# A decoder layer on one core: constants placed later, activation tables ordered, head sums in two float32r parts, values turned and then centred

## The chip, the core and the metric

The kernel runs on one core of one Trainium2 chip. The metric is the device time of one execution in microseconds (us), the median of several runs. The engines are PE (TensorE, matmuls; PEld is its weight load), DVE (VectorE), ACT (ScalarE), POOL (GpSimd) and SP (SyncE, here the queue of most DMAs). Each engine runs its own instructions strictly in the order in which they stand; engines wait for one another by semaphores.

## The reference

One decoder layer over 256 tokens of width 2048 in float32: a SwiGLU feed-forward, a mixer (sliding-window attention beside an RWKV-7 time mix), cross-attention to a memory of 256 rows, a second feed-forward, a final norm. What the change touches is in the time mix and in attention's softmax (cut):

```python
kk = k * k_k
kk = kk / jnp.maximum(jnp.sqrt(jnp.sum(kk * kk, axis=-1, keepdims=True)), 1e-12)   # over 64
k = k * (1.0 + (a - 1.0) * k_a)
y = rwkv7_scan(r, decay, k, v, -kk, kk * a)
mean = jnp.mean(y, axis=-1, keepdims=True)
var = jnp.mean(jnp.square(y - mean), axis=-1, keepdims=True)
y = ((y - mean) * lax.rsqrt(var + GN_EPS)).reshape(B, T, RWKV_WIDTH) * ln_w + ln_b
bonus = jnp.sum(r * k * r_k, axis=-1, keepdims=True) * v
y = (y + bonus.reshape(B, T, RWKV_WIDTH)) * g
```

A head has 64 features. Three sums over a head's features are formed: of `kk * kk`, of `r * k * r_k`, and of `y * y` (with `y` centred).

## The kernel before

**Products.** Every large product takes its float32 operands as two float32r parts: `hi` (a copy rounded to float32r by ACT, L343) and `lo` (the rest, by DVE, L344), and adds three float32r matmuls, hi x hi, lo x hi, hi x lo (L436, L437, L438). Weights stream from HBM in tiles `raw` of 2 x 128 rows by 512 columns (`load`, by SP's queue); `next_item` hands out one tile after the other, loads ahead and has the next two split (`AHEAD = 2`). One such tile is 12 matmuls on PE: two row blocks, two halves of the tokens, three parts. `feed_forward` runs over three groups of columns with seven-product combinations in place of eight (L363 to L370); its first block ends with Silu at L603.

**Background work.** All else (norms, transposes, softmax, the time mix) is written as generators in groups (`Interleave`): after every few matmuls `bg.tick()` moves each group on by one `yield`; `idle(n)` lets n ticks pass, `wait_for(name)` waits for a flag. That gives the program's order. A scheduler then places the instructions on each engine by its own costs; where `tc.issue_after(ins)` is written, what follows stays behind that instruction. A load of an activation table is put ahead of an activation whose function the table in place lacks.

**The steps touched.**
- Start: POOL makes `ones`, `ident`, masks, `bdones` (ones in two 64x64 blocks), `bdmean` (1/64 there), `bdup` (2^40 there); DVE makes `center = ident - bdmean` (L243). POOL issues DMAs for `sinks`, `g_later`, `v_rwkv` (L249, L254); ACT copies one element (L859), which brings its first table.
- `attend`: scores of 4 or 8 heads on PE (L932, L179), maxima on DVE (L959), exponentials on ACT (L965), sums and quotients on DVE (L972 to L975), `idle(4)`, transposes on PE (L187), products with `vt` (L179).
- `decay_and_rate`: per half h of the heads, products with `wa` on PE, Sigmoid on ACT (L1104), a scan on DVE (L1111), then Exp three times (L1125, L1129, L1130) and L1132.
- `removal_keys(h)`: `kk`, its square on ACT (L1148), two fp32 matmuls with `bdones` (L1153), Sqrt on ACT (L1154), reciprocals on DVE, and the products for the inverse.
- `substitute` and `invert` form the inverse of a triangular matrix in blocks: products of `xb` and `rb` (L1319), a copy `n` by ACT (L1356), products of `n` and `xu` (L1319), copies into `xb`.
- `values(h)`: eight fp32 matmuls with `center` (L1272) turn the values to tokens on partitions and centre them per head; ACT copies them to `vtok` (L1276); two fp32 matmuls with `bdones` (L1279) sum `kt` (which by then holds r * k * r_k); DVE multiplies that by the values (L1285).
- `chain(h)`: `masked` (products and a mask by DVE, L1411), `known` (L1421, copied by ACT to `u`, L1432), `solved` (L1438, L1443), `results`; `finish(h)`: square (L1517), two fp32 matmuls with `bdmean` (L1522), Sqrt (L1523), reciprocals, gate products (L1533), `yr`.

Of the kernel before, what the change touches and what calls it, by code (L numbers as in the profile page):

```python
# [142 lines left out]
def decoder_layer(ctx: ExitStack, tc: tile.TileContext, a: dict, out: bass.AP):  # L143
# [19 lines left out]
    def f32(x):  # L163
        return x.bitcast(F32)
# [57 lines left out]
    ups = cpool.tile([P, P], F32, name="ups")  # L222
    pool.memset(ups[:], UP)
    mask3 = cpool.tile([P, 3, P], F32, name="mask3")
    select(mask3[:, 0, :], ups[:], [[1, P]], ALU.is_gt, 0.0, 0, -1)
    select(mask3[:, 1, :], ups[:], [[1, P]], ALU.is_ge, 0.0, 0, -1)
    select(mask3[:, 2, :], ups[:], [[1, P]], ALU.is_ge, 0.0, 0, -1)

    mask_l = cpool.tile([P, P], F32, name="mask_l")
    select(mask_l[:], ups[:], [[-1, P]], ALU.is_gt, 0.0, 0, 1)  # L230
    bdones = cpool.tile([P, P], F32, name="bdones")
    bdmean = cpool.tile([P, P], F32, name="bdmean")
    bdup = cpool.tile([P, P], F32, name="bdup")
    pool.memset(bdones[:], 0.0)
    pool.memset(bdmean[:], 0.0)
    pool.memset(bdup[:], 0.0)
    for e in range(2):
        q = slice(64 * e, 64 * e + 64)
        pool.memset(bdones[q, q], 1.0)
        pool.memset(bdmean[q, q], 1.0 / 64)  # L240
        pool.memset(bdup[q, q], UP)
    center = cpool.tile([P, P], F32, name="center")
    dve.tensor_tensor(center[:], ident[:], bdmean[:], ALU.subtract)  # L243
# [5 lines left out]
    pool.dma_start(sinks[:], a["attn_sinks"].broadcast_to([P, 16]))  # L249
# [590 lines left out]
    with tc.tile_pool(name="f1", bufs=1, reuse_waits="tile") as sp:  # L840
        aligned(sp)
        at["pool"] = sp
        x = sp.tile([P, 2, D], F32, name="x")

        def col(n):
            return x[:, :, n * 512 : (n + 1) * 512]

        n1 = Norm(g_ffn1)
        turned = [sp.tile([P, 4, T], F32, tag="hb", name="xt", bufs=2) for _ in range(2)]
        pair = sp.tile([P, 8, T], F32, tag="thi", name="xt")  # L850
        turned = [v[:] for v in turned] + [pair[:, :4], pair[:, 4:]]
# [36 lines left out]


    with tc.tile_pool(name="mx", bufs=1, reuse_waits="tile") as sp:  # L890
# [28 lines left out]
        def attend(kvs, qb):  # L919
# [55 lines left out]
            dve.tensor_tensor(  # L975
                s3, s3, den[:].unsqueeze(2).to_broadcast([P, n, w]), ALU.mult
            )
            yield from idle(4)
            pt = t4("pt", (P, 2, 4, P))
            b = two()  # L980
            turn(
# [97 lines left out]
        def decay_and_rate():  # L1079
# [8 lines left out]
            for h in range(2):  # L1088
                cs.append(t4("cs"))
                aa.append(t4("aa"))  # L1090
                for q in (0, 2):
                    b = two()
                    by_turns(
                        (
                            b[:, e, i * T : (i + 1) * T],
                            wa[64 * e : 64 * e + 64, (4 * h + q + i) * P : (4 * h + q + i + 1) * P],
                            xwa[64 * e : 64 * e + 64, :],
                        )
                        for i in range(2) for e in (1, 0)
                    )  # L1100
                    for i in range(2):
                        for e, (dst, bias) in enumerate(((cs[h], w0), (aa[h], a0))):
                            c = 4 * h + q + i
                            act.activation(  # L1104
                                dst[:, q + i, :], b[:, e, i * T : (i + 1) * T], AF.Sigmoid,
                                bias=bias[:, c : c + 1],
                            )
                yield from idle(4)
            for h in range(2):
# [25 lines left out]

        bg.spawn("ew", decay_and_rate())
        kt = []

        def removal_keys(h):
            yield from wait_for(f"k{h}")  # L1140
# [6 lines left out]
            yield  # L1147
            act.activation(sq[:], kk[:], AF.Square)  # L1148
            yield
            b = two()  # L1150
            v = sq[:].rearrange("p (a c) t -> p a (c t)", a=2)
            for i in range(2):
                pe.matmul(b[:, i], bdones[:], v[:, i], start=True, stop=True)  # L1153
# [111 lines left out]
        def values(h):  # L1265
            yield from wait_for(f"v{h}")
            vv = bv[h]
            vtok.append(t4("vtok", (P, 2, 512)))
            b = two()
            for c in range(2):  # L1270
                for j in range(4):
                    pe.matmul(  # L1272
                        b[:, c, j * P : (j + 1) * P], vv[:, j, c * P : (c + 1) * P], center[:],
                        start=True, stop=True,
                    )
            act.copy(vtok[h][:], b[:])  # L1276
            b = two()
            for i in range(2):
                pe.matmul(  # L1279
                    b[:, i], bdones[:],  # L1280
                    kt[h][:, 2 * i : 2 * i + 2, :].rearrange("p c t -> p (c t)"),
                    start=True, stop=True,
                )
            v2 = vv[:].rearrange("p (a c) t -> p a (c t)", a=2)
            dve.tensor_tensor(v2, b[:], v2, ALU.mult)  # L1285
            yield
            bg.seen.add(f"ready{h}")

# [217 lines left out]
        def finish(h):  # L1506
# [7 lines left out]
            pool.dma_start(g2[96:, 1, :], W["rwkv_g2"][P:, f4])  # L1514
            y = yq[h]
            sq = room("sq", (P, 4, T))
            act.activation(sq[:], y[:], AF.Square)  # L1517
            yield
            b = two()
            v = sq[:].rearrange("p (a c) t -> p a (c t)", a=2)  # L1520
            for i in range(2):
                pe.matmul(b[:, i], bdmean[:], v[:, i], start=True, stop=True)  # L1522
            act.activation(v, b[:], AF.Sqrt, bias=gneps[:])  # L1523
            yield
            for i in range(4):
                dve.reciprocal(sq[:, i], sq[:, i])
# [267 lines left out]
```

## Time and profile before

| what | us |
|---|---|
| median of 3 runs (lowest, highest) | 2230.0 (2228.66, 2230.67) |
| the profiled execution | 2228.26 |
| its span, first to last instruction | 2226.5 |
| PE busy; DVE; ACT; POOL | 2212.4; 1746.7; 1193.4; 70.9 |
| mean granted TensorE clock | 0.999 |

The profile is of one execution. A timeline row reads: start, length, engine, line, operation, output <- inputs, partitions x elements, and in brackets the idle time ahead of the row and what ended it; an fp32 matmul leaves two records. A row of waits reads: who waited for whom, then the total, the number of waits and the longest. A row of stretches gives the busy time of each engine in a window.

### The profile page before, as it was taken

How to read it: one execution, taken by the hardware profiler on the slowest of the kernel's cores; microseconds unless marked ns; L12 is line 12 of the kernel's file. 1: busy time of each engine (PE TensorE's matmuls, PEld its weight loads, DVE VectorE, ACT ScalarE, POOL GpSimd, SP SyncE). 2: the span in 40 equal slices, each digit the busy share in tenths (PEclk: the TensorE clock that was granted, in tenths of full speed). 3: DMA queues.
4: the chain of work that ended last, by engine and by line, in shares of the span. 5: the costliest groups of instructions: out<-in, count | busy, mean ns of one | idle time of the engine just before them, and what ended most of it. 6: DMA issues, size and time to landing. Idle time of an engine off the chain costs nothing.

```text
span 2226.5 us, 28338 instructions
## 1 busy us (share of the span) xinstructions
PE 2212.4 (99%) x10790; PEld 1820.2 (82%) x10790; DVE 1746.7 (78%) x2038; ACT 1193.4 (54%) x1436; POOL 70.9 (3%) x139
## 2 busy tenths in 40 slices
PE   9999999999999999999999999999999999999998
PEld 7788888888888877888888888888888888888886
DVE  7988988898887567977556476558888988898887
ACT  6555555555555557544434445556555555555554
POOL 1000000000000000010400000000000000000000
PEclk9999999999999999999999999999999999999999
DMA  7566665565656544677524766557665665565564
GB/s 260 199 220 194 206 206 191 189 208 192 205 188 216 163 138 150 211 231 223 170 64 148 236 218 205 183 166 260 202 202 184 206 203 194 189 208 191 206 206 153
DMA packets 220536, 433.31 MB, mean 195 GB/s; under 512 B 13952, under 2 KB 16336, under 8 KB 220400
## 3 DMA queue, kind: packets, MB, share of 16 engines
q1 hardware_dynamic: 213200, 410.70, 55.7%
q0 software_dynamic: 6624, 20.14, 2.9%
q8 instruction: 84, 1.38, 0.3%
q10 hardware_dynamic: 576, 0.66, 0.1%
q14 instruction: 52, 0.43, 0.1%
HBM read 419.00 MB, written 12.45 MB: 194 GB/s over the span
## 4 chain that ended last, share of the span: by engine, by line
PE 97%; DVE 1%; ACT 1%; DMA 0%; issue 0%; POOLq 0%; POOL 0%; SPq 0%; ACTq 0%; DVEq 0%
PE acc L436 21%; PE acc L437 21%; PE acc L438 21%; PE two L437 9%; PE two L436 9%; PE two L438 9%; PE two L187 2%; PE two L179 1%; PE two L1319 0%; DVE lo L344 0%; PE acc L1456 0%; DMA raw<-in_ffn_w_up_dram 0%; PE acc L1438 0%; PE acc L1421 0%; PE two L1533 0%
## 5 line engine op out<-in xcount | busy, mean ns | idle before, releaser
L343 ACT CAST hi<-raw 128x1024 fp32r<-128x1024 f32 (+1 forms) x769 | 763.3, 1002 | 788.5 <-PE two L438 369.8
L344 DVE TENSOR_TENSOR lo<-raw,hi 128x1024 fp32r<-128x1024 f32 (+1 forms) x770 | 882.9, 1156 | 331.3 <-ACT hi L343 330.1
L436 PE MATMUL acc<-hi,xhi 128*128 128x512 f32 (+1 forms) x1224 | 479.4, 393 | 2.3 <-ACT hi L343 2.0
L437 PE MATMUL acc<-lo,xhi 128*128 128x512 f32 (+1 forms) x1224 | 474.8, 388 | 0.8 <-DVE lo L344 0.8
L438 PE MATMUL acc<-hi,xlo 128*128 128x512 f32 (+1 forms) x1224 | 474.0, 387 | 0.0
L436 PEld LDWEIGHTS acc<-hi,xhi 128*128 128x128 f32 x1224 | 229.7, 188 | 55.6 <-issue 5.1
L437 PEld LDWEIGHTS acc<-lo,xhi 128*128 128x128 f32 x1224 | 229.9, 188 | 49.8 <-DVE lo L344 2.8
L438 PEld LDWEIGHTS acc<-hi,xlo 128*128 128x128 f32 x1224 | 229.8, 188 | 46.3 <-DVE xlo L710 0.2
L369 DVE TENSOR_TENSOR tlo<-raw,thi 128x1024 fp32r<-128x1024 f32 x160 | 192.8, 1218 | 0.0
L368 ACT CAST thi<-raw 128x1024 fp32r<-128x1024 f32 x160 | 165.7, 1050 | 33.6 <-DVE raw L363 19.3
L437 PE MATMUL acc<-lo,hhi 128*128 128x512 f32 x424 | 166.4, 392 | 0.0
L438 PE MATMUL acc<-hi,hlo 128*128 128x512 f32 x424 | 165.2, 390 | 0.0
L436 PE MATMUL acc<-hi,hhi 128*128 128x512 f32 x424 | 159.9, 391 | 0.0
L436 PE MATMUL two<-hi,xhi 128*128 128x512 f32 x352 | 138.4, 393 | 0.0
L438 PE MATMUL two<-hi,xlo 128*128 128x512 f32 x352 | 137.1, 390 | 0.0
L437 PE MATMUL two<-lo,xhi 128*128 128x512 f32 x352 | 137.1, 389 | 0.0
L363 DVE TENSOR_TENSOR raw<-raw 128x1024 f32<-128x1024 f32 x80 | 97.4, 1217 | 14.9 <-DMA raw<-in_ffn_w_up_dram 13.8
L437 PEld LDWEIGHTS acc<-lo,hhi 128*128 128x128 f32 x424 | 79.6, 188 | 19.2 <-DVE lo L344 3.0
L436 PEld LDWEIGHTS acc<-hi,hhi 128*128 128x128 f32 x424 | 79.1, 188 | 18.9 <-ACT hi L343 2.6
L438 PEld LDWEIGHTS acc<-hi,hlo 128*128 128x128 f32 x424 | 79.6, 188 | 16.2
L436 PEld LDWEIGHTS two<-hi,xhi 128*128 128x128 f32 x352 | 66.1, 188 | 15.0 <-DVE u L588 0.5
L438 PEld LDWEIGHTS two<-hi,xlo 128*128 128x128 f32 x352 | 66.0, 188 | 13.8
(385 smaller groups left out, 3181.6 us busy)
## 6 DMA issues: line engine op xcount, KB each, us to landing
raw<-in_ffn_w_gate_dram SPq DMA_DIRECT2D x171, 512.0 KB, 3.7
raw<-in_ffn_w_up_dram SPq DMA_DIRECT2D x167, 512.0 KB, 4.6
raw<-in_ffn_w_down_dram SPq DMA_DIRECT2D x152, 512.0 KB, 4.7
raw<-in_w_in_dram SPq DMA_DIRECT2D x136, 512.0 KB, 3.6
raw<-in_w_out_dram SPq DMA_DIRECT2D x32, 512.0 KB, 4.2
raw<-in_ffn_w_down_dram SPq DMA_DIRECT2D x12, 1024.0 KB, 5.1
raw<-in_w_proj_attn_dram SPq DMA_DIRECT2D x16, 512.0 KB, 3.8
raw<-in_w_proj_rwkv_dram SPq DMA_DIRECT2D x16, 512.0 KB, 4.3
```

Of the source, the lines that this page charges most:

```text
L179: prev = pe.matmul(to, lhs, rhs, **how)
L187: prev = pe.transpose(to, src, ident[:])
L343: newest["act"] = act.copy(hi[:, s], raw[:, s])
L344: newest["dve"] = dve.tensor_tensor(lo[:, s], raw[:, s], f32(hi[:, s]), ALU.subtract)
L363: dve.tensor_tensor(ta[:], raw[:, 1:3], raw[:, 0:2], ALU.subtract)
L368: act.copy(hi[:, s], t[:])
L369: dve.tensor_tensor(lo[:, s], t[:], f32(hi[:, s]), ALU.subtract)
L436: pe.matmul(o, xh, hi, start=first, stop=False, **how)
L437: pe.matmul(o, xh, lo, start=False, stop=False, **how)
L438: newest["pe"] = pe.matmul(o, xl, hi, start=False, stop=last, **how)
```

## The change

**Constants.** The DMAs for `g_later`, `v_rwkv` and `sinks` move into the generator `late_vectors`, behind `idle(60)`. The masks are selected in place of from `ups`; `bdones` and `bdmean` become float32r; `center` goes.

**Tables.** The first activation is a Silu instead of a copy. After the copy of `q0` to `qt` a one-element Exp follows. The Exps of `decay_and_rate` are held behind the last Sigmoid. One `idle(4)` in `attend` becomes `idle(5)`.

**Head sums.** `head_sums` adds two float32r matmuls, of a high part and a low part, in place of one fp32 matmul. The high part comes from ACT (a second Square, or a copy), the low part from DVE. The parts have one buffer each (`bufs=1`), and `alone()` lets one user in at a time.

**Values.** `values` turns with transposes, then DVE sums 64 features per head and token (`vmean`) and adds -1/64 of it.

```diff
+    def by_head(name, value, dt):
+        t = cpool.tile([P, P], dt, name=name)
+        pool.memset(f32(t[:]), 0.0)
...
+    bdones = by_head("bdones", 1.0, F32R)
+    bdmean = by_head("bdmean", 1.0 / 64, F32R)
...
-    pool.dma_start(sinks[:], a["attn_sinks"].broadcast_to([P, 16]))
-    gains = vectors("g_later", 4 * KD, pool)
-    rv = vectors("v_rwkv", 83, pool)
...
     def late_vectors():
+        yield from idle(60)
+        pool.dma_start(gains[:], a["g_later"])
+        pool.dma_start(rv[:], a["v_rwkv"])
+        pool.dma_start(sinks[:], a["attn_sinks"].broadcast_to([P, 16]))
         yield from idle(20)
...
-        act.copy(junk_t[:, :1], ones[:, :1])
+        act.activation(junk_t[:, :1], ones[:, :1], AF.Silu)
...
-            act.copy(dst[:], feats(tok))
+            last = act.copy(dst[:], feats(tok))
+            if name == "q0":
+                with tc.issue_after(last.ins):
+                    act.activation(junk_t[:, :1], ones[:, :1], AF.Exp)
...
-            yield from idle(4)
+            yield from idle(5 if nk == 2 and kvs[0] else 4)
...
-                act.activation(dec[h][:], dec[h][:], AF.Exp, scale=-DECAY)
-                act.activation(e0[h][:], mid[:], AF.Exp, scale=DECAY)
-                act.activation(ee[h][:], c3, AF.Exp, scale=-DECAY)
+                with tc.issue_after(rates.ins):
+                    act.activation(dec[h][:], dec[h][:], AF.Exp, scale=-DECAY)
+                    act.activation(e0[h][:], mid[:], AF.Exp, scale=DECAY)
+                    act.activation(ee[h][:], c3, AF.Exp, scale=-DECAY)
...
+        def head_sums(bd, parts):
+            b = two()
+            for i in range(2):
+                for j, part in enumerate(parts):
+                    pe.matmul(b[:, i], bd[:], part[:, i], start=j == 0, stop=j == 1)
+            return b
+        def alone():
+            while "parts" in bg.seen:
+                yield
+            bg.seen.add("parts")
...
+            yield from alone()
+            parts = parted("sq")
+            act.activation(parts[0][:], wide4(kk), AF.Square)
             act.activation(sq[:], kk[:], AF.Square)
             yield
-            for i in range(2):
-                pe.matmul(b[:, i], bdones[:], v[:, i], start=True, stop=True)
-            act.activation(v, b[:], AF.Sqrt)
+            dve.tensor_tensor(parts[1][:], v, f32(parts[0][:]), ALU.subtract)
+            yield from idle(2)
+            act.activation(v, head_sums(bdones, parts)[:], AF.Sqrt)
+            bg.seen.discard("parts")
...
-                    pe.matmul(
-                        b[:, c, j * P : (j + 1) * P], vv[:, j, c * P : (c + 1) * P], center[:],
-                        start=True, stop=True,
+                    pe.transpose(
+                        b[:, c, j * P : (j + 1) * P], vv[:, j, c * P : (c + 1) * P], ident[:]
                     )
-            act.copy(vtok[h][:], b[:])
+            dve.tensor_reduce(vmean[h][:], b3, AX.X, ALU.add)
+            dve.scalar_tensor_tensor(
+                vtok[h][:].rearrange("p c (g f) -> p (c g) f", f=64),
+                vmean[h][:].unsqueeze(2).to_broadcast([P, 16, 64]), -1.0 / 64, b3,
+                ALU.mult, ALU.add,
+            )
+            parts = parted("sq")
+            act.copy(parts[0][:], wide4(kt[h]))
+            dve.tensor_tensor(parts[1][:], wide4(kt[h]), f32(parts[0][:]), ALU.subtract)
+            yield from idle(2)
+            dve.tensor_tensor(wide4(vv), head_sums(bdones, parts)[:], wide4(vv), ALU.mult)
```

`finish` is changed as `removal_keys` is, with `bdmean`.

**Where instructions stand.** Line numbers of the changed kernel are higher by 2 (start) to 32 (chain): its L345/L346 are the casts `hi` and `lo` (L343/L344 before), L438 to L440 the three matmuls, L1154 the matmul of `head_sums`, L1351 those of `invert`.

PE, the first inversion and the start of the first chain, before; `xb`, `rb`, `n`, `xu` are the inverse's tiles, `at`, `rt`, `aa`, `kk` those of `masked`, `vtok` and `mk` those of `known`:

```order
L1319 MATMUL two<-xb,rb 64x64 x15
L179 MATMUL two<-at,aa 128x128 x4
L437 MATMUL acc<-lo,xhi 128x512
L179 MATMUL two<-rt,aa 128x128 x8
L1319 MATMUL two<-n_8933,xu 64x64 x16
L438 MATMUL acc<-hi,xlo 128x512
L436 MATMUL acc<-hi,xhi 128x512
L437 MATMUL acc<-lo,xhi 128x512
L438 MATMUL acc<-hi,xlo 128x512
L1421 MATMUL acc<-vtok,mk 128x64 x8
```

and of the change:

```order
L1351 MATMUL two<-xb,rb 64x64 x15
L438 MATMUL acc<-hi,xhi 128x512
L439 MATMUL acc<-lo,xhi 128x512
L440 MATMUL acc<-hi,xlo 128x512
L1351 MATMUL two<-n_8989,xu 64x64 x16
L179 MATMUL two<-at,aa 128x128 x8
L179 MATMUL two<-rt,aa 128x128 x8
L1453 MATMUL acc<-vtok,mk 128x64 x8
```

The products of `masked`, which stood around the products with `rb`, now stand behind those with `xu`, right ahead of `known`.

DVE, the first softmax, between the sums of the exponentials and the quotients, before:

```order
L344 TENSOR_TENSOR lo<-raw,hi 128x1024
L974 RECIPROCAL den<-den 128x8
L974 RECIPROCAL den<-den 128x4
L975 TENSOR_TENSOR s<-s,den 128x1024 x2
L344 TENSOR_TENSOR lo<-raw,hi 128x1024 x2
```

and of the change:

```order
L346 TENSOR_TENSOR lo<-raw,hi 128x1024
L979 RECIPROCAL den<-den 128x8
L979 RECIPROCAL den<-den 128x4
L346 TENSOR_TENSOR lo<-raw,hi 128x1024
L980 TENSOR_TENSOR s<-s,den 128x1024 x2
```

One more `lo` stands ahead of the quotients; on PE the transposes behind them stand eight matmuls later. On ACT the load of Exp's table and the one-element Exp stand ahead of the cast `hi` which before stood ahead of the load.

POOL, the end of its start, of the change, with what each waits for in brackets:

```order
L245 MEMSET keep 128x2 [waits Pool_49]
L274 MEMSET gneps 128x1
L276 MEMSET nhalf 128x2
L266 DMA g_later<-in_g_later_dram 128x64
L267 DMA v_rwkv<-in_v_rwkv_dram 128x83
L268 DMA sinks<-in_attn_sinks_dram 128x16
L756 TENSOR_TENSOR rs<-ms,nhalf 128x2 [waits DVE_49,Pool_49]
```

Before, the three stood among the last memsets, ahead of `gneps`; now they stand behind all of them and ahead of the first wait for another engine.

More of the change, by code (lines that the diff above doesn't have):

```diff
@@ L220, in decoder_layer @@
     select(abias[:, 1, :], abias[:, 1, :], [[-1, P]], ALU.is_ge, NEG, 0, 1)
-    ups = cpool.tile([P, P], F32, name="ups")
-    pool.memset(ups[:], UP)
     mask3 = cpool.tile([P, 3, P], F32, name="mask3")
-    select(mask3[:, 0, :], ups[:], [[1, P]], ALU.is_gt, 0.0, 0, -1)
-    select(mask3[:, 1, :], ups[:], [[1, P]], ALU.is_ge, 0.0, 0, -1)
-    select(mask3[:, 2, :], ups[:], [[1, P]], ALU.is_ge, 0.0, 0, -1)
+    pool.memset(mask3[:], UP)
+    for m, op in enumerate((ALU.is_gt, ALU.is_ge, ALU.is_ge)):
+        select(mask3[:, m, :], mask3[:, m, :], [[1, P]], op, 0.0, 0, -1)
     mask_l = cpool.tile([P, P], F32, name="mask_l")
[L230 to L243, printed above, removed]
+    pool.memset(mask_l[:], UP)
+    select(mask_l[:], mask_l[:], [[-1, P]], ALU.is_gt, 0.0, 0, 1)
+    def by_head(name, value, dt):
+        t = cpool.tile([P, P], dt, name=name)
+        pool.memset(f32(t[:]), 0.0)
+        for e in range(2):
+            q = slice(64 * e, 64 * e + 64)
+            pool.memset(f32(t[q, q]), value)
+        return t
+    bdones = by_head("bdones", 1.0, F32R)
+    bdmean = by_head("bdmean", 1.0 / 64, F32R)
+    bdup = by_head("bdup", UP, F32)
+    vmean = [cpool.tile([P, 16], F32, name="vmean") for _ in range(2)]
     keep = cpool.tile([P, 2, P], F32, name="keep")
@@ L257, in decoder_layer @@
     g_ffn1 = vectors("g_first", KD, act)
-    gains = vectors("g_later", 4 * KD, pool)
+    gains = cpool.tile([P, 4 * KD], F32, name="g_later")
     g_mix, g_cross, g_mem, g_ffn2 = (gains[:, i * KD : (i + 1) * KD] for i in range(4))
-    rv = vectors("v_rwkv", 83, pool)
+    rv = cpool.tile([P, 83], F32, name="v_rwkv")
     w0, a0, k_k, k_a, r_k, ln_w, ln_b = (rv[:, i * 8 : (i + 1) * 8] for i in range(7))
@@ L1103, in decay_and_rate @@
                             c = 4 * h + q + i
-                            act.activation(
+                            rates = act.activation(
                                 dst[:, q + i, :], b[:, e, i * T : (i + 1) * T], AF.Sigmoid,
@@ L1137, in decoder_layer, with parted, wide4 @@
         kt = []
+        def parted(name):
+            return [
+                sp.tile([P, 2, 512], F32R, tag=name + e, name=name + e, bufs=1)
+                for e in ("hi", "lo")
+            ]
+        def head_sums(bd, parts):
[8 more added lines that the diff above has]
+            bg.seen.add("parts")
+        def wide4(x):
+            return x[:].rearrange("p (a c) t -> p a (c t)", a=2)
         def removal_keys(h):
@@ L1271, in values @@
                 for j in range(4):
-                    pe.matmul(
-                        b[:, c, j * P : (j + 1) * P], vv[:, j, c * P : (c + 1) * P], center[:],
-                        start=True, stop=True,
-                    )
-            act.copy(vtok[h][:], b[:])
[L1277 to L1285, printed above, removed]
+                    pe.transpose(
+                        b[:, c, j * P : (j + 1) * P], vv[:, j, c * P : (c + 1) * P], ident[:]
+                    )
+            b3 = b[:].rearrange("p c (g f) -> p (c g) f", f=64)
+            dve.tensor_reduce(vmean[h][:], b3, AX.X, ALU.add)
[4 more added lines that the diff above has]
+            )
+            yield from alone()
+            parts = parted("sq")
[3 more added lines that the diff above has]
+            dve.tensor_tensor(wide4(vv), head_sums(bdones, parts)[:], wide4(vv), ALU.mult)
+            bg.seen.discard("parts")
             yield
@@ L1516, in finish @@
             sq = room("sq", (P, 4, T))
+            v = wide4(sq)
+            yield from alone()
+            parts = parted("sq")
+            act.activation(parts[0][:], wide4(y), AF.Square)
             act.activation(sq[:], y[:], AF.Square)
             yield
[L1519 to L1523, printed above, removed]
+            dve.tensor_tensor(parts[1][:], v, f32(parts[0][:]), ALU.subtract)
+            yield from idle(2)
+            act.activation(v, head_sums(bdmean, parts)[:], AF.Sqrt, bias=gneps[:])
+            bg.seen.discard("parts")
             yield
```

3 lines of the change are left out of this document (1 added, 2 removed).

## The prediction

> **What bounds the kernel.** I read the page first, for the busy shares.
>
> ```profile
> span 2226.5 us, 28338 instructions
> PE 2212.4 (99%) x10790; PEld 1820.2 (82%) x10790; DVE 1746.7 (78%) x2038; ACT 1193.4 (54%) x1436; POOL 70.9 (3%) x139
> ```
>
> TensorE is busy for 99% of the span, so nearly every microsecond of its work that goes is a microsecond of the kernel. The view of waits, for TensorE alone, says how little else there is:
>
> ```profile
> PE acc L436 <- ACT hi L343: 2.0, 2, 1.3
> PE two L187 <- DVE s L975: 1.2, 2, 0.9
> PE acc L204 <- POOL ones L199: 1.1, 1, 1.1
> PE acc L437 <- DVE lo L344: 0.8, 2, 0.5
> PE two L187 <- ACT tok L905: 0.4, 1, 0.4
> PE acc L436 <- ACT xhi L709: 0.3, 1, 0.3
> ```
>
> These waits sum to 5.8 us (total, times, longest). The rest of the change (tables, constants) can win at most the part of them that it touches. The sum is made against the profiled execution, 2228.26 us; the shown runs have a median of 2230.0, so I carry the difference over to that median.
>
> **Sums over a head, and values.** Matmul records overlap, so a block is priced from its start to the start of what follows, in the timeline of TensorE. First the pace of float32r work and of eight transposes:
>
> ```profile
> 1062.12 0.40 PE L437 MATMUL acc<-lo,xhi 128*128 128x512 f32 x1
> ...
> 1083.66 1.03 PE L187 MATMUL two<-ident,tok 128*128 128x128 f32 x8
> 1084.45 0.48 PE L436 MATMUL acc<-hi,xhi 128*128 128x512 f32 x1
> 1084.77 0.40 PE L437 MATMUL acc<-lo,xhi 128*128 128x512 f32 x1
> ```
>
> Between the first two rows lie eight weight tiles of 12 matmuls less one, 95: 21.54 / 95 = 0.227 us each. Eight transposes take 0.79, and the matmul behind them 0.32 instead of 0.227: 0.88 in all. Then the blocks that the change replaces, the sum of squares of the removal keys (two fp32 matmuls, four records) and the values (eight matmuls with `center`, then two with `bdones`):
>
> ```profile
> 873.54 1.88 PE L1153 MATMUL two<-sq,bdones 128*128 128x512 f32 x4
> 874.86 0.80 PE L436 MATMUL acc<-hi,xhi 128*128 128x512 f32 x1
> 875.49 0.40 PE L437 MATMUL acc<-lo,xhi 128*128 128x512 f32 x1
> ...
> 1158.33 1.95 PE L1272 MATMUL two<-center,bv 128*128 128x128 f32 x16
> ...
> 1161.43 0.79 PE L436 MATMUL acc<-hi,xhi 128*128 128x512 f32 x1
> 1162.06 0.40 PE L437 MATMUL acc<-lo,xhi 128*128 128x512 f32 x1
> ```
>
> A head sum costs 875.49 - 873.54 - 0.227 = 1.72 us, the values 1162.06 - 1158.33 - 0.227 = 3.50. Before: four head sums alone (two of keys, two of group norm, of the same shape) and two of values, 4 x 1.72 + 2 x 3.50 = 13.9. After: six head sums of four float32r matmuls, 6 x 4 x 0.227 = 5.4, and two times eight transposes, 1.8: 7.2. TensorE is rid of **6.7 us**, 6.3 if each new block costs one more change of kind (0.09 on the way in).
>
> VectorE and ScalarE pay. VectorE gets ten more passes over 128x1024 (six low parts, two means, two subtractions), 10 x 1.22 = 12 us by the rows of the chain below; ScalarE six more and two copies fewer, about 4 us, and three table loads fewer. Both have room in these stages:
>
> ```profile
> 860.00:960.00 100.00, 100.00 (x480) 80.57 (x479) 80.52 (x82) 54.81 (x60) 8.15 (x14) 1.00 0.66 208
> 1088.00:1130.00 42.00, 41.98 (x488) 34.98 (x487) 19.64 (x24) 13.70 (x19) 6.20 (x12) 1.00 0.30 92
> ```
>
> (stretch, length, then busy us of PE, PEld, DVE, ACT, POOL.) VectorE is at 81% in the stage of the keys and 47% in the chain, ScalarE at 55% and 33%. So these passes cost nothing but where TensorE stands right behind one.
>
> It does at one place, the first inversion and chain, whose new order is shown above.
>
> ```profile
> 1106.46 0.71 PE L179 MATMUL two<-at,aa 64*128 64x128 f32 x8
> 1107.10 0.50 PE L437 MATMUL acc<-lo,xhi 128*128 128x512 f32 x1
> ...
> 1108.71 0.50 PE L1319 MATMUL two<-n,xu 64*64 64x64 f32 x5
> ...
> 1106.56 1.01 ACT L1356 COPY n<-two 64x1024 f32<-64x1024 f32 x1 [1.66 <-PE two L1319]
> ...
> 1107.22 1.22 DVE L1411 TENSOR_TENSOR mk<-two,mask 128x1024 f32<-128x1024 f32 x1 [1.87 <-PE two L179]
> ```
>
> Now: the products with `rb` end at 1106.46, ScalarE copies them until 1107.57, and the next products start at 1108.71, behind 2.25 us of other work. In the new order only three float32r matmuls stand between, 3 x 0.227 + 0.09 = 0.77, against 0.10 + 1.01 + about 0.1 that the copy takes: a wait of about 0.4. Then `masked` takes 0.12 + 1.22 + about 0.1 behind its products, and only eight short ones (1.09 us) stand before `known`: 0.3 more. I take **+0.7**; zero if the records flatter these ends, 3 if each of the chain's eight hand-overs loses as much (8 x 0.35). What waits behind is only filler of the gate product, and nothing else is late: the last `yr` part keeps more than ten weight tiles before the product that reads it.
>
> **Tables.** Three of 17 loads go. One is seen by TensorE:
>
> ```profile
> 50.75 1.28 ACT L603 ACT_TABLE_LOAD   x1
> 52.05 0.69 ACT L603 ACTIVATE hb<-acc,rs 128x512 f32<-128x512 f32 x1
> ...
> 53.72 1.04 ACT L343 CAST hi<-raw 128x1024 fp32r<-128x1024 f32 x1
> ...
> 53.27 0.69 DVE L484 TENSOR_TENSOR clo<-u,chi 128x512 fp32r<-128x512 f32 x1 [0.96 <-ACT chi L481]
> ...
> 55.48 1.22 DVE L344 TENSOR_TENSOR lo<-raw,hi 128x1024 fp32r<-128x1024 f32 x1
> ...
> 54.82 0.74 PE L436 MATMUL acc<-hi,xhi 128*128 128x512 f32 x2 [0.70 <-ACT hi L343]
> ...
> 56.75 0.50 PE L437 MATMUL acc<-lo,xhi 128*128 128x512 f32 x1 [0.49 <-DVE lo L344]
> ```
>
> The load of Silu's table holds the cast `hi` back by 1.28, which costs TensorE 0.70, and then 0.49 for `lo`. Without it `hi` is in time; `lo` stands on VectorE behind L484 and what follows it, which sat idle 0.96 for `chi`, itself behind the load. So `lo` comes about 1.0 earlier for a TensorE that comes 0.7 earlier: 0.2 of its wait stays. **-1.0**, at most -1.2, zero if `lo` is held by the passes before it. The Trainium skill (ScalarE: Activation LUTs, What ACT_TABLE_LOAD costs) counts 1.28 us for the load and 1.38 for a drain; the rows show 1.30 from the load's start to the next ACTIVATE, so the trace disagrees on the drain. By that section of the Trainium skill both waits would go whole, 1.2 instead of 1.0, and the sum would be 0.2 lower.
>
> In attention the new load of Exp's table moves work too.
>
> ```profile
> 766.87 1.05 ACT L343 CAST hi<-raw 128x1024 fp32r<-128x1024 f32 x1 [0.37 <-PE acc L438]
> 770.79 1.28 ACT L965 ACT_TABLE_LOAD   x1 [2.87 <-DVE es L962]
> ...
> 779.94 2.36 DVE L975 TENSOR_TENSOR s<-s,den 128x1024 f32<-128x1024 f32 x2
> ...
> 781.31 1.06 PE L187 MATMUL two<-ident,s 128*128 128x128 f32 x8 [0.86 <-DVE s L975]
> ...
> 817.65 1.21 DVE L975 TENSOR_TENSOR s<-s,den 128x1024 f32<-128x1024 f32 x1
> ...
> 818.98 1.04 PE L187 MATMUL two<-ident,s 128*128 128x128 f32 x8
> ```
>
> Before, the load stood in a gap of 2.87 us. Now it stands, with a dummy Exp, before the cast of 766.87, which starts about 1.1 later; its `lo` and both maxima queue behind it on VectorE, so the exponentials start about 0.95 later although no load is ahead of them. One more `lo` (1.15 net of overlap) stands before L975, and the transposes come eight matmuls (1.8) later: 0.86 + 0.95 + 1.15 - 1.8, about 1.15, 0.3 worse. The second wait on L975 (1.2 - 0.9 = 0.3) goes, since those transposes come six matmuls later. At 818.98 there was no wait, with 0.12 to spare behind L975; there one more 128x1024 `lo` is ahead of it (1.2) and TensorE comes 0.3 later: 0.75 new. The wait on `tok` (0.4) stays, 0.1 longer: less table, but six matmuls less ahead. Together **+0.8**; -1.6 if all these waits go, +2.5 if two more softmaxes lose a `lo`.
>
> **Constants.** The three DMAs are written later, but they wait for nothing and POOL has nothing before them to wait for, so POOL issues them right behind its memsets, later than now by the few short memsets that stand ahead (an estimate: 0.7 us), and past no other queue's work.
>
> ```profile
> 4.99 0.73 POOL L249 DMA_DIRECT2D sinks<-in_attn_sinks_dram  x1
> ...
> 11.71 1.99 ACT L343 CAST hi<-raw 128x1024 fp32r<-128x1024 f32 x2 [3.08 <-DMA raw<-in_ffn_w_up_dram]
> ```
>
> They share the DMA engines with the second weight tile in either order, which lands at 11.71. I take **0**, between +0.3 and -1.6 (the 1.3 on `hi` and 0.3 on `lo` that TensorE loses there). The masks, `bdones` and `center` are made under the first products: 0; without that cover some 0.5.
>
> **Sum:** -6.7 + 0.7 - 1.0 + 0.8 + 0 = -6.2, so 2222.1 for a profiled run and **2223.8 us** for the median.
>
> **Rivals.** (1) *The waits go as well*: attention loses its waits (-1.6 instead of +0.8) or the chain none: a further 0.7 (chain) to 3.1 us (both), 2220.7 to 2223.1 and about 2221. For it: the scheduler left no wait in the chain before. Against: it placed table loads and casts wrongly by 0.3 to 0.9 us before. 12%. (2) *The constants are late indeed*, and the first tile lands for an unstalled TensorE: a further -1.6, 2222.2, inside the forecast's range. The Trainium skill (DMA: Bandwidth & Descriptors, Queues, rings and completion order) has each engine take turns between queues, which no run here shows for these. 6%. (3) *VectorE gives the gain back*: its extra passes stand before `lo` in the stage of the keys, where it is at 81%, so a third to a half of the 12 us reaches TensorE: 2223.8 + 2 to 5, about 2227. Against: weights are split two tiles, 5.4 us, ahead. 14%. (4) *Slower*: the head sums' new path in the chain (cast, subtract, sums, multiply, each on another engine) becomes the bound. It decides once the ten added passes fall on TensorE's path in full, with 0.1 of hand-over each: 13 instead of 0.7, so 2223.8 + 12.5, about 2236. For it: between 1100 and 1112 few float32r matmuls fill. Against: the scheduler hoists the casts many tiles ahead. 5%. The forecast keeps 63%.
>
> **Chances.** This kernel's runs can tell some 0.2%, 4.5 us, from no change: below 2225.5 is faster, above 2234.5 slower. The forecast's own range from its terms' bounds is 2220.5 to 2227. With (1) and (2) nearly all of it is faster: 0.82; (3) and the forecast's upper end give the same, 0.13; (4) slower, 0.05. The range takes in (1) and most of (3): **2219.5 to 2228**.
>
> **What would show it.** In the profile after: blocks of four 512-wide matmuls with `bdones` or `bdmean` of 0.91 us from start to next start (wrong if near 1.7); eight transposes of the values in 0.8 to 0.9; no load and no wait near 54; waits on the softmax near 783 and 820 of about 1; two waits under 0.5 near the first chain; the constants' DMAs on POOL between 5 and 8 us and the same 1.3 wait near 12.8. It would be wrong if TensorE's waits in 860 to 1225 sum to over 3 us, or if the span fell by more than TensorE's busy time plus 3.

## The result, and the profile after

The changed kernel takes 2221.75 us (median of 6 runs, 2220.58 to 2223.26) against 2229.44 for the kernel before (6 runs): ratio 0.9965, interval 0.9952 to 0.9978, so 7.7 us less, 4.9 to 10.7. The profiled execution took 2222.56, with a span of 2220.8 against 2226.5: 5.7 less. The forecast was 2223.8 (6.2 less), in a range of 2219.5 to 2228.

The head of the page of the changed kernel, and its view of TensorE's waits (total, times, longest):

```profile
span 2220.8 us, 28313 instructions
PE 2207.0 (99%) x10774; PEld 1817.7 (82%) x10774; DVE 1759.2 (79%) x2047; ACT 1193.8 (54%) x1438; POOL 72.0 (3%) x140
...
PE acc L204 <- POOL ones L199: 1.1, 1, 1.1
PE two L187 <- ACT tok L907: 1.0, 2, 0.6
PE acc L439 <- DVE lo L346: 0.9, 2, 0.6
PE acc L438 <- ACT hi L345: 0.7, 2, 0.5
PE two L187 <- DVE s L980: 0.6, 1, 0.6
PE acc L438 <- ACT xhi L711: 0.4, 1, 0.4
PE two L1351 <- ACT n L1388: 0.2, 1, 0.2
PE two L438 <- DVE hlo L669: 0.2, 1, 0.2
```

TensorE is busy for 5.4 us less (2212.4 to 2207.0), VectorE for 12.5 more, as the forecast counted (12). The waits sum to 5.1 instead of 5.8, but they stand in other places. Both executions, cut at the same three pieces of work (the transposes of `tok` that begin attention, end it and end the mixer), show where the 5.7 came from. The columns are the stretch, its length, the busy time of PE, PEld, DVE, ACT and POOL with the number of records, then TensorE's granted clock, the DMA engines' busy share and their GB/s; first the kernel before, then the changed one:

```profile
0.00:764.42 764.42, 760.24 (x3403) 624.94 (x3404) 644.04 (x744) 420.69 (x485) 11.67 (x39) 1.00 0.61 205
764.42:853.51 89.09, 87.53 (x515) 68.12 (x514) 62.39 (x96) 57.84 (x108) 1.22 (x3) 1.00 0.44 133
853.51:1435.99 582.48, 582.46 (x3360) 482.35 (x3361) 384.58 (x442) 285.31 (x337) 48.21 (x82) 1.00 0.59 187
1435.99:2226.50 790.51, 782.13 (x3515) 644.77 (x3513) 655.67 (x757) 429.57 (x509) 9.80 (x15) 1.00 0.58 198
```

```profile
0.00:763.43 763.43, 760.76 (x3402) 624.83 (x3403) 644.11 (x743) 419.76 (x484) 12.22 (x40) 1.00 0.61 205
763.43:852.92 89.49, 87.77 (x516) 68.18 (x514) 60.95 (x95) 55.16 (x105) 1.21 (x3) 1.00 0.43 132
852.92:1430.28 577.36, 576.33 (x3344) 480.09 (x3345) 398.24 (x453) 289.16 (x343) 48.70 (x82) 1.00 0.59 188
1430.28:2220.80 790.52, 782.15 (x3515) 644.56 (x3513) 655.87 (x757) 429.72 (x509) 9.82 (x15) 1.00 0.58 198
```

The first feed-forward gives 0.99, attention costs 0.40, the time mix gives 5.12, the rest 0. In the time mix VectorE does 13.7 us more and TensorE 6.1 less. A head sum and the transposes of the values look like this in the timeline of TensorE:

```profile
877.90 0.40 PE L1154 MATMUL two<-sqhi,bdones 128*128 128x512 f32 x1
878.13 0.40 PE L1154 MATMUL two<-sqlo,bdones 128*128 128x512 f32 x1
878.37 0.39 PE L1154 MATMUL two<-sqhi,bdones 128*128 128x512 f32 x1
878.60 0.39 PE L1154 MATMUL two<-sqlo,bdones 128*128 128x512 f32 x1
878.83 0.40 PE L438 MATMUL acc<-hi,xhi 128*128 128x512 f32 x1
...
1097.21 1.04 PE L1301 MATMUL two<-ident,bv 128*128 128x128 f32 x8
1098.01 0.48 PE L438 MATMUL acc<-hi,xhi 128*128 128x512 f32 x1
1098.32 0.40 PE L439 MATMUL acc<-lo,xhi 128*128 128x512 f32 x1
```

The sum takes 878.83 - 877.90 = 0.93 in place of 1.72, the transposes 1098.32 - 1097.21 - 0.23 = 0.88.

One wait, 0.59 for `tok` at 1036.94, stands in this profile alone: in the four later profiles of kernels that keep this part or add to VectorE's work in it (E, G, H and I below) the same stage took 576.43 to 576.45 instead of 577.36, without that wait. So the change is worth about 6.0 us there. Why this one execution had the wait isn't known.

### The profile page after: what moved, and what is told of

The parts are those of the page before. It is cut to its first block, busy times and chain, and to the rows that moved or that the text cites. A ratio compares the mean times of both kernels' runs of the same rounds, so it can differ in the third digit from the quotient of the medians.

```text
span 2220.8 us, 28313 instructions
## 1 busy us (share of the span) xinstructions
PE 2207.0 (99%) x10774; PEld 1817.7 (82%) x10774; DVE 1759.2 (79%) x2047; ACT 1193.8 (54%) x1438; POOL 72.0 (3%) x140
## 3 DMA queue, kind: packets, MB, share of 16 engines
q8 instruction: 84, 1.38, 0.2%
## 4 chain that ended last, share of the span: by engine, by line
PE 96%; DVE 1%; issue 1%; ACT 1%; DMA 0%; POOLq 0%; POOL 0%; SPq 0%; ACTq 0%; DVEq 0%
PE acc L438 21%; PE acc L439 20%; PE acc L440 20%; PE two L438 9%; PE two L439 9%; PE two L440 9%; PE two L187 2%; PE two L179 1%; DVE lo L346 1%; PE two L1351 0%; PE acc L1488 0%; PE acc L1453 0%; PE acc L1470 0%; PE two L1568 0%; PE acc L1351 0%
## 5 line engine op out<-in xcount | busy, mean ns | idle before, releaser
L345 ACT CAST hi<-raw 128x1024 fp32r<-128x1024 f32 (+1 forms) x769 | 764.0, 1003 | 794.3 <-PE two L440 370.6
L346 DVE TENSOR_TENSOR lo<-raw,hi 128x1024 fp32r<-128x1024 f32 (+1 forms) x770 | 884.2, 1158 | 325.0 <-ACT hi L345 323.7
L438 PE MATMUL acc<-hi,xhi 128*128 128x512 f32 (+1 forms) x1224 | 477.9, 391 | 1.1 <-ACT hi L345 0.7
L440 PE MATMUL acc<-hi,xlo 128*128 128x512 f32 (+1 forms) x1224 | 473.8, 387 | 0.0
L438 PEld LDWEIGHTS acc<-hi,xhi 128*128 128x128 f32 x1224 | 229.6, 188 | 53.3 <-issue 3.9
L440 PEld LDWEIGHTS acc<-hi,xlo 128*128 128x128 f32 x1224 | 229.8, 188 | 46.3 <-DVE xlo L712 0.2
L440 PE MATMUL acc<-hi,hlo 128*128 128x512 f32 x424 | 165.1, 389 | 0.0
L438 PE MATMUL acc<-hi,hhi 128*128 128x512 f32 x424 | 159.8, 391 | 0.1
L438 PE MATMUL two<-hi,xhi 128*128 128x512 f32 x352 | 138.4, 393 | 0.0
L440 PE MATMUL two<-hi,xlo 128*128 128x512 f32 x352 | 137.0, 389 | 0.0
L438 PEld LDWEIGHTS acc<-hi,hhi 128*128 128x128 f32 x424 | 79.1, 188 | 18.8 <-ACT hi L345 2.6
L440 PEld LDWEIGHTS acc<-hi,hlo 128*128 128x128 f32 x424 | 79.6, 188 | 16.3
L438 PEld LDWEIGHTS two<-hi,xhi 128*128 128x128 f32 x352 | 66.1, 188 | 15.0 <-DVE u L590 0.5
L440 PEld LDWEIGHTS two<-hi,xlo 128*128 128x128 f32 x352 | 66.1, 188 | 13.9
```

The lines of the kernel that those rows point to most:

```text
L345: newest["act"] = act.copy(hi[:, s], raw[:, s])
L346: newest["dve"] = dve.tensor_tensor(lo[:, s], raw[:, s], f32(hi[:, s]), ALU.subtract)
L438: pe.matmul(o, xh, hi, start=first, stop=False, **how)
L440: newest["pe"] = pe.matmul(o, xl, hi, start=False, stop=last, **how)
```

## Experiments

Differences are of medians, each against the runs of the kernel before on the same chip (2229.4 for A to H, 2230.3 for I and J).

| kernel | median | change | ratio, interval |
|---|---|---|---|
| A sums and values alone | 2223.61 | -5.8 | 0.9975, 0.9964 to 0.9985 |
| B values alone | 2227.84 | -1.5 | 0.9992, 0.9984 to 1.0001 |
| C tables alone | 2228.45 | -0.9 | 0.9996, 0.9987 to 1.0005 |
| D constants alone | 2228.65 | -0.7 | 0.9997, 0.9988 to 1.0006 |
| E the change, constants at 92 us | 2221.65 | -7.8 | 0.9963, 0.9949 to 0.9977 |
| F before, sinks' DMA last | 2229.29 | -0.1 | 0.9998, 0.9989 to 1.0007 |
| G the change, low parts twice | 2221.36 | -8.1 | 0.9962, 0.9950 to 0.9975 |
| H the change, Exp's table earlier | 2220.88 | -8.6 | 0.9960, 0.9947 to 0.9972 |
| I as H, one more idle | 2220.31 | -10.0 | 0.9954, 0.9942 to 0.9967 |
| J the change without the idles | 2223.48 | -6.8 | 0.9968, 0.9956 to 0.9981 |

**A. Sums and values alone.** The kernel before with `head_sums`, its six users and the new `values`; `bdones` and `bdmean` become float32r in their old places.

> The kernel before with the head sums in two float32r parts and the values turned and centred; constants and tables stay. Theory (TensorE's time is rid of the fp32 matmuls, and the ten passes on VectorE are hidden): 5.4 to 6.2 us less, a median near 2223.6, and TensorE's waits in the stages of the keys and of the chain under 0.5 us. Rival (VectorE gives the gain back): 1.5 to 4 us less, with waits on lo or on the low parts of 2 us or more. Rival (the hand-overs of the chain bound it): no gain or a loss.

5.8 us less. The stage from the keys to the end of the mixer took 577.50 instead of 582.48, with 1.1 us of waits in it (0.20 for `n`, 0.87 for `mk`). No wait on a low part. The time is the theory's and both rivals fall; the theory's bound of 0.5 us on the waits is passed by the one on `mk`, which B shows too.

**B. Values alone.**

```diff
-                    pe.matmul(
...
+                    pe.transpose(
...
-            act.copy(vtok[h][:], b[:])
...
+            dve.tensor_reduce(vmean[h][:], b3, AX.X, ALU.add)
+            dve.scalar_tensor_tensor(
...
```

> The kernel before with the values turned and centred alone; the sum of r * k * r_k behind them stays in fp32. Theory: two blocks of eight fp32 matmuls of 1.78 us become eight transposes of 0.88, so 1.8 us less in TensorE's time, a median near 2227.6. The forecast's own count (3.50 us for the values with the head sum behind them, 1.72 for a head sum alone) gives the same 1.8. Rival (the two new passes of VectorE between the transposes and the chain's first product are waited for): 0 to 0.8 us less, with a wait on vtok.

TensorE's busy time in the stage fell from 582.46 to 580.67, the 1.8 expected. But one wait is new, in the timeline of TensorE (the chain of the second half):

```profile
1165.88 0.32 PE L1425 MATMUL acc<-vtok,mk 128*128 128x64 f32 x1 [0.92 <-DVE mk L1415]
```

So 0.9 of the 1.8 is given back in this profile: neither the theory nor the rival has it whole. The wait is not for `vtok` but for the mask's product, which starts on VectorE at 1164.66 behind other passes, among them the two new ones (1159.60 and 1161.87). The median's 1.5 can't decide, since its interval holds zero. With A, 1.8 of TensorE's gain is the values' and the rest the sums'.

**C. Tables alone.** The Silu, the Exp behind `q0`, the order of the Exps behind the Sigmoids and the idle of 5.

> The kernel before with the three edits on ACT's tables and the idle of 5; all else stays. Theory (the trace after): the two waits near 55 go for the most part and 0.3 to 0.5 us come back within 40 us behind them; in attention waits move but their sum stays: 0.3 to 0.9 us less in all. Forecast: 1.0 less and 0.8 more, 0.2 less in all, waits on the softmax of 1.1 and 0.75. Rival (the load with a drain): 1.2 less at the start.

The first stage took 763.47 (764.42 before), attention 89.41 (89.09): 0.6 less in these two stages, though the whole span was 0.2 longer (2226.7), by the last stage. The medians' 0.9 less has an interval that holds zero. So the time decides nothing; the rows speak for the theory. Behind the two waits near 55 TensorE is 0.97 earlier (57.60 instead of 58.57), and after a wait of 0.23 for `hlo` at 60.84 it is 0.45 earlier (61.17 instead of 61.62): the rival's 1.2 without a return isn't there.

**D, E, F. Constants.** D has the change's masks and later DMAs alone. E and F:

```diff
 # E, the change with
-        pool.dma_start(gains[:], a["g_later"])
-        pool.dma_start(rv[:], a["v_rwkv"])
-        pool.dma_start(sinks[:], a["attn_sinks"].broadcast_to([P, 16]))
+        with tc.issue_after(newest["load"].ins):
+            nc.sync.dma_start(gains[:], a["g_later"])
+            nc.sync.dma_start(rv[:], a["v_rwkv"])
+            nc.sync.dma_start(sinks[:], a["attn_sinks"].broadcast_to([P, 16]))
 # F, the kernel before with
-    pool.dma_start(sinks[:], a["attn_sinks"].broadcast_to([P, 16]))
...
     rv = vectors("v_rwkv", 83, pool)
+    pool.dma_start(sinks[:], a["attn_sinks"].broadcast_to([P, 16]))
```

> The kernel before with the constants' three DMAs written later and the masks made as in the change; sums, values and tables stay. Theory (the later issue of the sinks' DMA takes a stall out of the weight stream near 10 us): the wait on hi near 12.8 falls from 1.27 to about 0.5 and the time by 0.8 us. Rival (the forecast: three DMAs of the same kind in the same window; the stall is a chance of that one profile): a wait of 0.5 or 1.3 by chance, no change of the time within 0.5.

> The changed kernel with the three DMAs of the constants on SP's queue behind the weight loads of that place, some 40 us after the start. Theory (these DMAs stall the weight stream near 10 us): no stall of the DMA engines between 9 and 12 us, the waits of 0.49 and 0.28 near 12 and 13 gone, 0.8 us less than the changed kernel (2221.0 against 2221.8). Rival (the second weight tile is bound by its own bytes): waits of 0.5 and 0.3 again and the same time.

> The kernel before with one line moved: the sinks' DMA stands behind the two of g_later and v_rwkv instead of ahead of them, so it is issued near 6.2 us instead of 4.99; nothing else. If the sinks' 16-element rows are what stalls the weight stream, the stall moves from 9.6 to about 11 us and the wait on hi near 12.8 falls from 1.27 to 0.5 to 0.8. If it is all three, the stall stays near 10 us and the wait at 1.2 or more. The time moves by under 0.8 us either way.

The busy share of the DMA engines over the first 16 us, in 40 slices of 0.4 us (a digit is tenths): of the kernel before, with the bandwidth of each slice below it, then of F, the changed kernel, D and E in this order; in the first four also the row of POOL's queue (packets, MB, share of the 16 engines' time):

```profile
DMA  0000368989999999999999999049999999999999
GB/s 0 0 0 0 56 129 306 376 259 371 348 371 369 356 356 287 287 266 333 364 384 405 410 343 67 0 164 406 421 436 384 394 410 405 410 389 420 379 415 410
q0 software_dynamic: 96, 0.08, 7.9%
...
DMA  0000368989999999999999999997598999999999
q0 software_dynamic: 96, 0.08, 5.4%
...
DMA  0000568979999999899999999999999999999999
q0 software_dynamic: 96, 0.08, 1.7%
...
DMA  0000559989999999999999999999996989999999
q0 software_dynamic: 96, 0.08, 4.4%
...
DMA  0000648999999999999999999999999999999999
```

Before, the stream falls to 67, 0 and 164 GB/s in the slices from 9.6 to 10.8, and POOL's 96 packets take 7.9% of the engines' time; A, B and C, with the old order too, have 8.3, 7.4 and 7.7%. The queue's row for the one microsecond from 9 to 10 tells what holds the engines:

```profile
q0 software_dynamic: 16, 0.01, 104.7%
```

Sixteen packets, 0.01 MB in all as the sinks' 8 KB would be, took 104.7% of what 16 engines have in that microsecond: about a microsecond of an engine each. In F the sinks' DMA is issued last, at 6.31 instead of 4.99, with the other two ahead of it, and the dent is later too, from 10.8 to 11.6; in E, without the three, there is none. So the dent goes with the sinks' DMA. The Trainium skill (DMA: Bandwidth & Descriptors, Queues, rings and completion order) lets an engine take turns between queues by whole packets. The rows agree in that the weights stand still while such packets last; the packet's microsecond is the measurement's.

The later issue doesn't always make these packets short. With the sinks issued at 7.2 the queue's share is 1.7% in the changed kernel and in G, but 2.3 to 4.4% in J, I, H and D, and in D the stream still falls to 146 GB/s, now between 11.2 and 12.4. What the later issue does in all six is to put the dent, where there is one, behind the landing of the second weight tile.

What the dent costs is seen in that landing, read from ScalarE's first cast of the tile: 11.71, 12.02, 11.75 and 11.77 in the four kernels with the old order (before, A, B, C), 11.59 in F, 10.67 to 11.24 in the six that issue the DMAs later (D, the changed kernel, G, H, I, J), and 10.92 in E. TensorE starts its products with the tile at 12.80 to 13.12 in the first four, 12.69 in F, 11.77 to 12.34 in the six and 12.02 in E. The wait on `hi` ahead of them is a poorer measure, since TensorE doesn't come to it at the same time: 1.27 before, but 0.71 in C with the old order. F's 0.63 is what its expectation gave for the sinks, yet TensorE gains 0.11 there; F settles where the dent comes from, not what it costs. D's wait was 0.74, the changed kernel's 0.49, and E's still 0.40, though its constants were issued at 92.31, later than the 40 us that were meant. So E's rival holds: with no constants in the way the tile is no earlier than in the six, and moving them yet later brings nothing. And the 0.59 that D gained at 12 us (12.21 instead of 12.80) doesn't reach the end: D's first stage took 764.44, as before, and its median is 0.7 lower with an interval from 2.7 lower to 1.3 higher, which leaves both theory and rival of D open as to the time. In D a wait of 0.55 on a `lo` at 19.30 took it back at once; what does so in the others wasn't settled, since first stages of the same start differ by up to 1.9 us from run to run (762.30 to 764.23).

**G. Low parts twice.** Each of the six subtractions is written twice.

```diff
             dve.tensor_tensor(parts[1][:], v, f32(parts[0][:]), ALU.subtract)
+            dve.tensor_tensor(parts[1][:], v, f32(parts[0][:]), ALU.subtract)
```

> The changed kernel with each of the six low parts of the head sums formed twice (the same subtraction into the same tile), which is 6 x 1.22 = 7.3 us more on VectorE in the stages of the keys and of the chain, and nothing else. Theory (VectorE's passes are hidden): within 0.5 us of the changed kernel, with the wait on tok near 1037 of 0.6 grown to at most 1. Rival (a third to a half reaches TensorE): 2.4 to 3.7 us more.

The stage of the changed kernel (first row) and of G:

```profile
852.92:1430.28 577.36, 576.33 (x3344) 480.09 (x3345) 398.24 (x453) 289.16 (x343) 48.70 (x82) 1.00 0.59 188
...
851.72:1428.16 576.44, 576.00 (x3344) 480.25 (x3345) 404.41 (x459) 289.17 (x343) 48.70 (x82) 1.00 0.62 189
```

VectorE does 6.2 us more in six instructions more, the stage is not longer, and no wait is new; the one on `tok` near 1037, which the expectation let grow, isn't there. The cover is read off the changed kernel's rows: the first low part is formed at 869.44, and the sum that reads it starts at 877.90.

```profile
869.44 1.23 DVE L1180 TENSOR_TENSOR sqlo<-sq,sqhi 128x1024 fp32r<-128x1024 f32 x1 [0.68 <-ACT sq L1178]
```

**H, I. Attention.** H loads Exp's table behind another copy; I also changes one idle.

```diff
 # H and I
-            if name == "q0":
+            if name == "kv":
 # I alone
-            yield from idle(5 if nk == 2 and kvs[0] else 4)
+            yield from idle(5 if kvs[0] == 2 else 4)
```

> The changed kernel with the one-element Exp behind the copy of kv instead of that of q0, some 22 us earlier, where ScalarE idles 1.66 us between casts. Theory (the load delays the cast ahead of the maxima by 1.1, and the softmax with it): the exponentials start 1.0 earlier, the waits of 0.60 and 0.61 near 778 and 819 go for the most part: 0.8 to 1.2 us less than the changed kernel. Rival (VectorE's passes ahead of the quotients set these waits): under 0.3 us less, waits in the same places.

> The changed kernel with the one-element Exp behind the copy of kv, and the idle of 5 also given to the single head group that follows (kvs[0] == 2), which puts its eight transposes two matmuls later. Theory: the wait of 0.60 near 818 shrinks by 2 x 0.23 to about 0.15, no other wait grows: 0.4 to 0.5 less than with the preload alone (2220.4 against 2220.9), 1.3 less than the changed kernel. Rival (the products behind the transposes are waited for instead): no change against the preload alone.

The changed kernel's load, the cast that it delays, the first exponential, the three waits of the stage (ScalarE and TensorE):

```profile
765.54 1.28 ACT L917 ACT_TABLE_LOAD   x1
766.84 0.20 ACT L917 ACTIVATE junk<-ones 128x1 bf16<-128x1 f32 x1
766.95 1.03 ACT L345 CAST hi<-raw 128x1024 fp32r<-128x1024 f32 x1
771.88 2.91 ACT L970 ACTIVATE s<-two,nm 128x128 f32<-128x128 f32 x10 [3.90 <-DVE es L967]
778.35 0.50 PE L439 MATMUL acc<-lo,xhi 128*128 128x512 f32 x1 [0.60 <-DVE lo L346]
818.81 1.06 PE L187 MATMUL two<-ident,s 128*128 128x128 f32 x8 [0.61 <-DVE s L980]
852.92 1.09 PE L187 MATMUL two<-ident,tok 128*128 128x128 f32 x8 [0.44 <-ACT tok L907]
```

and of H, whose attention also starts at 763.43:

```profile
742.87 1.28 ACT L917 ACT_TABLE_LOAD   x1
769.82 2.18 ACT L970 ACTIVATE s<-two,nm 128x128 f32<-128x128 f32 x8 [2.89 <-DVE es L967]
817.85 1.06 PE L187 MATMUL two<-ident,s 128*128 128x128 f32 x8 [0.60 <-DVE s L980]
```

The exponentials start 2.06 earlier (the theory had 1.0), the wait at 778 is gone, and attention takes 88.49 instead of 89.49. The wait near 818 stays at 0.60: there the rival is right, VectorE's passes ahead of the quotients set it. In I, whose transposes come two matmuls later, it is 0.34, and attention takes 87.89. Theory and rival each had one wait. I has the lowest median of all kernels tried; its interval and the changed kernel's overlap, so only the trace tells them apart.

**J. Without the idles.** `yield from idle(2)` ahead of each head sum goes (three places, six sums).

> The changed kernel without the idle of 2 between the low part and the head sum at its three places (six sums in all). It asks what hides the path square, square, subtract (1.0 + 1.0 + 1.2 us) ahead of each sum. Theory (the matmuls that the two ticks leave between hide it): TensorE waits 0.5 to 2 us at each of the sums, 3 to 10 us more than the changed kernel. Rival (the scheduler, which orders by its own costs, keeps work between in any case): within 0.7 us of the changed kernel and no new wait over 0.5.

No sum waits. The first one starts at 875.04, its low part (870.19) long done: the scheduler leaves work between of its own accord. The stage takes 577.03, 0.6 more than in E, G, H and I; its one wait of weight is in the second chain, while the 0.2 for `n` is gone:

```profile
1163.31 0.88 PE L1451 MATMUL acc<-vtok,mk 128*128 128x64 f32 x6 [0.91 <-DVE mk L1441]
```

It is the wait of A and B, from another order. By the ratios J is 0.7 us behind the changed kernel, inside the intervals, as the rival had it but for the one wait.

## Why the prediction held, step by step

| term | forecast | trace |
|---|---|---|
| sums and values on TensorE | -6.7 | -6.5 |
| waits and restarts in the chain | +0.7 | +0.4 |
| Silu's table | -1.0 | -0.5 to -0.8 |
| attention | +0.8 | +0.4 |
| constants | 0 | -0.8 at 12 us; in D 0 at the end of the stage |

The first two rows are the busy time and the rest of the stage in E, G, H and I (582.46 to 576.0, and 0.02 to 0.44). They give -6.0 in sum, just the forecast's, though each is smaller than forecast. The third is what stands at 60 us in the changed kernel (below), and C's first stage, 763.47, against 764.42, 764.47 and 763.83 in the three executions with the old start (before, A, B), mean 764.24; such stages scatter by as much. Silu's gain came out 0.2 to 0.5 smaller than forecast and attention's loss 0.4 smaller: that these two misses cancel is luck, and so is a total this close to the forecast.

- **Sums and values** were priced right, block by block (0.93 for 0.91, 0.88 for 0.88). The missing 0.2 stands at the two sums with fp32 products beside them, 1.11 at 1108.55 and 1.03 at 1172.08; the other four take 0.93 or 0.94.
- **The chain** waits at the first of the two places named, 0.21 instead of 0.4; behind `masked` it doesn't wait in the changed order, though in A, B and J the second chain does, by 0.9. The mechanism was right; the size depends on an order that the forecast could only read for one kernel.
- **Silu's table:** the direct gain is as forecast. Against its old place TensorE stands 1.81 earlier at 56.76, of which 0.78 had come by 12.02: 1.03. C is 0.97 earlier at the same row, having come 0.07 later to its place near 12.8: 1.04. The forecast missed what was late next: the products at 59.98, which wait for `hlo` and didn't wait before (61.39).

```profile
53.54 0.73 PE L438 MATMUL acc<-hi,xhi 128*128 128x512 f32 x2 [0.21 <-ACT hi L345]
56.76 0.48 PE L438 MATMUL two<-thi,chi 128*128 128x512 f32 x1
58.70 1.22 DVE L669 TENSOR_TENSOR hlo<-two,hhi 128x1024 fp32r<-128x1024 f32 x1
59.98 0.50 PE L438 MATMUL two<-hi,chi 128*128 128x512 f32 x1 [0.20 <-DVE hlo L669]
```

  One row further on TensorE is 1.3 earlier instead of 1.8 (0.2 of wait and the start again behind it). The Trainium skill (ScalarE: Activation LUTs, What ACT_TABLE_LOAD costs) counts a drain of 1.38 us beside the load of 1.28. The changed kernel's rows of 765.54 and 766.84, like those of before, show 1.30 from the load's start to the next ACTIVATE: no such drain shows here.
- **Attention:** the delay of the cast, and with it of the exponentials, was as argued (H shows it: the wait goes with the delay). But the forecast put the first wait at the transposes, 1.15; it came 3.8 us earlier, 0.60 at a `lo` that stands behind the sums of the exponentials on VectorE, and after it the transposes were in time. A lateness is paid where it is met first. The second, 0.75, was 0.61, and `tok` 0.44.
- **Constants:** the step that failed is that the DMAs "share the DMA engines with the second weight tile in either order", so that the wait of 1.3 stays. It fell to 0.49. The forecast had the issue times nearly right for two of the three, but the sinks went from first to last, 4.99 to 7.21, and it took all three for equal: in the old order the sinks' packets last a microsecond each and stand ahead of the tile's landing, in the new one they come behind it. The size was inside the bound (-1.6). In D the gain is lost again before the stage ends; in the changed kernel what is left of it can't be told from the scatter.
- **Rivals:** (1) the waits go as well: some did, some came. (2), the constants late and their stall gone, came true in part: the dent came behind the tile's landing, but that gave 0.8 at 12 us instead of 1.6, and E shows that no more is to be had. (3) is refuted by G, (4) by A and J.
- **Sums of the prediction:** three don't come out as written. The bounds of its terms, added up, give 2218.9 to 2229.5 and not 2220.5 to 2227; a third to a half of 12 us is 4 to 6 and not 2 to 5 (rival 3); and eight new blocks at 0.09 each would be 0.7 and not 0.4. The forecast of 2223.8 rests on none of them.

The forecast's 6.2 lies within the measured 4.9 to 10.7, which is too wide to judge the small terms. A, C and D together give 7.4, C and D with intervals that hold zero.

## What to carry to other kernels

Where one engine is busy for 99%, price each of its blocks from start to next start and count on that; here the sum was right to 0.2 us in 6.7, and the passes handed to an engine at 80% cost nothing as long as they stand microseconds ahead of their reader (in B two of them stood right ahead of a product that TensorE needed, and 0.9 came back). A stall that is taken away is worth only what the next late thing leaves: ask at each, and look at the order in which the waits are met. A DMA of a few bytes a row, issued while weights stream, need not be small: look at the share of the engines' time that its queue takes, not at its bytes, and at what lands behind it.

## What was not expected of the hardware

- The sinks' DMA, 8 KB in all, stopped the weight stream near 10 us, with about 1 us of an engine for each packet. The 96 packets of POOL's queue took 7.4 to 8.3% of the engines' first 16 us in the four profiles where it was issued at 4.99, 5.4% in F (6.31), and 1.7 to 4.4% in the six where it was issued at 7.2; why its packets last so differently wasn't tried.
- First stages of the same kernel start differ by up to 1.9 us (762.30 to 764.23), while the time mix repeats to 0.02 us in E, G, H and I (576.43 to 576.45); the changed kernel's own profile, at 577.36, is the exception.
